# The second of two modulation chunks in the attention stage is summed by VectorE instead of the tensor engine

## The chip, the cores and the metric

The kernel runs on one core of one Trainium2 chip. The metric is the device time of one execution in microseconds (us); the time of a kernel is the median of several runs. Engines are named as the profile names them: PE is TensorE's matrix products and PEld its weight loads, DVE is VectorE, ACT is ScalarE, POOL is GpSimd and SP is SyncE, whose queue starts nearly all transfers.

## The reference

The reference is a trunk of two layers over 256 latent tokens and 256 context tokens of width 1024, in float32. Layer 0 mixes by attention (four differential heads and eight grouped-query heads), layer 1 by a bidirectional state-space scan; each is followed by a gated feed-forward block with a short convolution.

What matters here is the modulation. For each layer a vector of six chunks of 1024 numbers is computed from a conditioning vector, once for the latent tokens and once for the context:

```
mod   = silu(c)     @ mod_w[layer] + mod_b[layer]
mod_c = silu(c_ctx) @ mod_w[layer] + mod_b[layer]
sh1, sc1, g1, sh2, sc2, g2 = split(mod, 6)
h = rms_norm(x) * (1 + sc1) + sh1        # before the mixer
x = x + g1 * mixer(h)
h = rms_norm(x) * (1 + sc2) + sh2        # before the feed-forward block
x = x + g2 * ffn(h)
```

A chunk is written (layer, number): (0,0) and (0,1) are sh1 and sc1 of layer 0, (0,2) is g1, (0,3) is sh2, (0,4) is sc2, (0,5) is g2. (0,2) is needed when the output projection of attention is added to x; (0,3) and (0,4) are needed at the start of the first feed-forward block.

## The kernel before

Activations lie with channels on the 128 partitions and the 512 tokens in the free dimension. Every large product is made with weight blocks of 128 x 128. Float32 weights are split into a rounded half and a rest (L237 on ACT, L238 on DVE), and so are the activations; a step of a large product is then three products of 512 columns (L294, L295, L296). Weights come from memory in units of 8 blocks, 512 KB each. A unit lands in one of 5 raw buffers and is split into one of 2 split buffers.

The work is a list of units that `plan` writes: "w" for a unit of weights, "m" and "d" for the 1024 columns of one modulation chunk over 128 of the 1024 input channels. A chunk therefore has 8 units, each of 512 KB. `load_raw` starts their transfers from SP in the order of the list, a few units ahead of their use. The function `merge` spreads one list evenly between the members of another, `run` at a time. `run_units` goes through a phase of the list:

- a "w" unit does 8 steps of the current large product;
- an "m" unit goes to `mod_piece` (L396): four products on PE, one for each 256 columns, placed in four column groups of 32. The weights are the conditioning vectors, the moving data is the raw unit. The profile records each of these float32 products twice, so a unit is 8 records;
- a "d" unit goes to `mod_dve`: for each of the two conditionings DVE multiplies the 128 x 1024 raw unit by the vector's number of each partition and adds it to a running sum `macc` (L413 for the first unit, L415 for the others). After the eighth unit, 8 products with `pick` on PE (L423, 16 records) add the partitions up into four groups of rows.

Both ways end in `mod_evac`: a copy out of PSUM (L510), two transposes (L514), the bias (L519) and, for chunks 1 and 4, the norm's gain (L522).

The attention input projection ("ai") has 18 units of weights. The first 6 make six blocks of columns together and belong to the start phase. The other 12 make one block of 128 columns each: keys (ka), queries (qa) and values (va) of the four differential heads, in the order ka0 qa0 va0 ka1 qa1 va1 ka2 qa2 ka3 qa3 va2 va3. When a block of queries is done, its head's steps are queued with due times on a clock that the code keeps: `self.now` grows by 645 with each step of a large product, by as much with each of a head's scores, and by 420 with each "m" unit, and `service` takes one due task after every step and every modulation unit. A head has three groups of scores (L980 on PE, maxima L995 on DVE, exponentials L1000 on ACT), then normalisation on DVE (L1016; L1024 and L1026), transposes (L1042), their copies (L1045 on DVE, L1047 on ACT) and the product with the values (L1062). The next stage, the output projection ("ao", 8 units), takes the heads' outputs, the last head's at the end.

The calls of the code give a program order; a list scheduler then orders each engine's instructions at compile time with the program order as priority and its own estimates of time. Loads, splits and score products have a raised priority. On the chip every engine works off its list in that fixed order. Tiles of one tag share a fixed number of buffers, so a transfer or an instruction that opens a tile waits until a buffer is free. In this stage `macc` shares the tag k (6 buffers) with the five split key tiles, and all modulation products share one bank of PSUM.

In the attention stage two chunks, (0,2) and (0,4), are "m" units, in runs of four between the 12 weight units; (0,3) is summed by DVE in the output projection, and the other chunks by DVE in later stages.

Of the kernel before, what the change touches and what calls it, by code (L numbers as in the profile page):

```python
# [144 lines left out]
class Trunk:  # L145
# [15 lines left out]
    def plan(self):  # L161
        def w(name):
            n = len(ORDERS[name]) // UB
            return [("w", name, i) for i in range(n)]

        def mod(*chunks):
            return [("m", c, k) for c in chunks for k in range(KD)]

        def merge(ws, ms, first=0, last=0, run=1):
            res, j = list(ws[:first]), 0  # L170
            body = ws[first:len(ws) - last]
            for i, u in enumerate(body):
                res.append(u)
                while j < len(ms) and j * len(body) < (i + 1) * len(ms):
                    res += ms[j:j + run]
                    j += run
            return res + list(ws[len(ws) - last:])

        ai = w("ai")
        start, n = [("s", 0, 0), ("s", 0, 1)], 0  # L180
        for k in range(KD):
            while n * UB < 6 * (k + 1):
                start.append(ai[n])
                n += 1
            if k + 1 < KD:
                start += [("s", k + 1, 0), ("s", k + 1, 1)]

        def dve(*chunks):
            return [("d", c, k) for c in chunks for k in range(KD)]
        self.ph = {}  # L190
        self.ph["start"] = start
        self.ph["ai"] = merge(ai[n:], mod((0, 2), (0, 4)), run=4)
        self.ph["ao"] = merge(w("ao"), dve((0, 3)), last=3)
        self.ph["f0i"] = merge(w("f0i"), dve((1, 0), (1, 1), (0, 5)), first=FIRST, last=4)
        self.ph["f0o"] = merge(w("f0o"), dve((1, 3), (1, 4), (1, 2)), first=2, last=4)
        self.ph["si"] = w("si")
        self.ph["so"] = w("so")
        self.ph["f1i"] = merge(w("f1i"), dve((1, 5)), first=FIRST, last=4)
        self.ph["f1o"] = w("f1o")
        for n in ("start", "ai", "ao", "f0i", "f0o", "si", "so", "f1i", "f1o"):  # L200
            self.units += self.ph[n]
# [1363 lines left out]
```

## Time and profile before

| what | value |
| --- | --- |
| median of 3 runs | 1148.45 us (1147.38 to 1149.57) |
| profiled execution, its own time | 1148.3 us |
| span from first to last instruction | 1146.5 us |
| granted clock of TensorE, mean | 0.997 |
| PE, DVE, ACT busy over the span | 98%, 73%, 53% |
| records of L396 (the "m" units) | 128, from 78.2 to 195.5 us |
| sums of chunk (0,3) on DVE | 198.1 to 235.7 us |

How to read it: a page of the profile gives busy time of each engine; a busy PE is not a PE at its peak, since its products overlap and their ends are modelled. The chain is the work that ended last, followed back from the last instruction to what released each step. A group of waits such as "ACT ws L237 <- PE ai L296: 9.2, 6, 4.2" means that ACT's instructions of line 237 stood idle for products of line 296 for 9.2 us in all, 6 times, 4.2 us at most. In rows of the timeline a bracket gives the idle time before an instruction and what ended it. A row of a tile gives the durations as lowest/median/highest in ns and the first and last start in us.

### The profile page before, as it was taken

The numbers are of one execution on the slowest core, as the hardware profiler recorded it, in microseconds if no ns is written. First come the engines' busy times: TensorE is split into PE (matmuls) and PEld (weight loads), VectorE is DVE, ScalarE is ACT, GpSimd is POOL, SyncE is SP. The second block draws the span as 40 slices with busy tenths as digits, with TensorE's granted clock in tenths as the row PEclk, the third lists the DMA queues.
The fourth block names the chain that finished last, engine by engine and source line by source line (L and its number), as shares of the span: only waits on it lengthen the run. The fifth ranks groups of instructions, "written<-read, shape, count | busy, mean of one in ns | idle before, by whom it ended". The sixth has DMA issues, their size and how long they took to land.

```text
span 1146.5 us, 17295 instructions
## 1 busy us (share of the span) xinstructions
PE 1126.7 (98%) x6662; PEld 923.5 (81%) x6662; DVE 834.8 (73%) x1395; ACT 608.4 (53%) x1088; POOL 27.0 (2%) x37
## 2 busy tenths in 40 slices
PE   8999999999999999999999999999999999999997
PEld 4676666679888888888788988888778899999985
DVE  4567777966776877846556479999888779877645
ACT  4366666644433333333222468987677559655533
POOL 0000000000000000000000000000000101000000
PEclk9999999999999999999999999999999999999999
DMA  7744133433354555536566324454344366776661
GB/s 276 263 152 138 42 110 121 141 107 93 110 168 145 170 167 160 184 93 193 174 205 238 95 85 135 123 160 127 120 138 133 107 178 221 262 224 201 184 194 45
DMA packets 55858, 177.13 MB, mean 154 GB/s; under 512 B 5792, under 2 KB 14304, under 8 KB 55648
## 3 DMA queue, kind: packets, MB, share of 16 engines
q1 hardware_dynamic: 55488, 175.51, 48.6%
q8 instruction: 52, 0.85, 0.3%
q10 hardware_dynamic: 288, 0.52, 0.1%
q14 instruction: 30, 0.25, 0.1%
HBM read 174.89 MB, written 1.11 MB: 154 GB/s over the span
## 4 chain that ended last, share of the span: by engine, by line
PE 89%; DVE 5%; ACT 3%; DMA 2%; issue 1%; SPq 0%; DVEq 0%; ACTq 0%
PE f0i L294 7%; PE f0i L296 7%; PE f0i L295 7%; PE f1o L453 5%; PE f1i L296 4%; PE f1i L295 4%; PE f1i L294 4%; PE si L294 3%; PE si L296 3%; PE si L295 3%; PE f0o L294 3%; PE ai L294 3%; PE f0o L296 3%; PE f0o L295 3%; PE ai L296 3%; PE ai L295 3%
## 5 line engine op out<-in xcount | busy, mean ns | idle before, releaser
L237 ACT ACTIVATE ws<-raw 128x1024 fp32r<-128x1024 f32 x215 | 226.6, 1056 | 252.2 <-PE f0i L296 90.5
L238 DVE TENSOR_TENSOR ws<-raw,ws 128x1024 fp32r<-128x1024 f32 x215 | 262.4, 1222 | 96.5 <-ACT ws L237 95.6
L415 DVE SCALAR_TENSOR_TENSOR macc<-raw,cpad,macc 128x1024 f32<-128x1024 f32 x84 | 106.7, 1280 | 35.1 <-DMA raw<-mod_w 34.8
L294 PE MATMUL f0i<-h,ws 128*128 128x512 f32 x336 | 131.4, 391 | 0.0
L295 PE MATMUL f0i<-h,ws 128*128 128x512 f32 x336 | 130.8, 389 | 0.0
L296 PE MATMUL f0i<-h,ws 128*128 128x512 f32 x336 | 130.8, 389 | 0.0
L294 PE MATMUL si<-h,ws 128*128 128x256 f32 (+1 forms) x312 | 109.9, 352 | 0.6 <-DVE cacc L1158 0.6
L296 PE MATMUL si<-h,ws 128*128 128x256 f32 (+1 forms) x312 | 105.2, 337 | 3.1 <-DVE ws L238 3.1
L295 PE MATMUL si<-h,ws 128*128 128x256 f32 (+1 forms) x312 | 105.6, 338 | 0.0
L294 PE MATMUL f1i<-h,ws 128*128 128x256 f32 x288 | 82.1, 285 | 0.0
L296 PE MATMUL f1i<-h,ws 128*128 128x256 f32 x288 | 82.0, 285 | 0.0
L295 PE MATMUL f1i<-h,ws 128*128 128x256 f32 x288 | 81.5, 283 | 0.0
L294 PEld LDWEIGHTS f0i<-h,ws 128*128 128x128 f32 x336 | 63.1, 188 | 14.1 <-ACT hid L664 0.8
L296 PEld LDWEIGHTS f0i<-h,ws 128*128 128x128 f32 x336 | 63.1, 188 | 13.2
L295 PEld LDWEIGHTS f0i<-h,ws 128*128 128x128 f32 x336 | 63.1, 188 | 13.0
L296 PEld LDWEIGHTS si<-h,ws 128*128 128x128 f32 x312 | 59.0, 189 | 11.2 <-DVE ws L238 5.0
L294 PEld LDWEIGHTS si<-h,ws 128*128 128x128 f32 x312 | 59.1, 189 | 10.8 <-issue 4.6
L295 PEld LDWEIGHTS si<-h,ws 128*128 128x128 f32 x312 | 59.2, 190 | 5.4
L453 PE MATMUL f1o<-ws,hid 128*128 128x512 f32 (+1 forms) x276 | 60.7, 382 | 0.0
L294 PE MATMUL f0o<-hid,ws 128*128 128x512 f32 x154 | 60.6, 393 | 0.0
L294 PE MATMUL ai<-h,ws 128*128 128x512 f32 x144 | 58.8, 422 | 1.6 <-ACT h L654 1.5
L296 PE MATMUL f0o<-hid,ws 128*128 128x512 f32 x154 | 60.1, 390 | 0.0
(315 smaller groups left out, 2479.6 us busy)
## 6 DMA issues: line engine op xcount, KB each, us to landing
raw<-mod_w SPq DMA_DIRECT2D x80, 512.0 KB, 4.2
raw<-w_f0i SPq DMA_DIRECT2D x44, 512.0 KB, 4.0
raw<-w_f1i SPq DMA_DIRECT2D x44, 512.0 KB, 4.3
raw<-w_si SPq DMA_DIRECT2D x41, 512.0 KB, 3.6
raw<-w_f0o SPq DMA_DIRECT2D x22, 512.0 KB, 4.4
raw<-w_f1o SPq DMA_DIRECT2D x22, 512.0 KB, 3.5
raw<-w_ai SPq DMA_DIRECT2D x18, 512.0 KB, 3.7
raw<-mod_s SPq DMA_DIRECT2D x16, 512.0 KB, 5.2
```

What stands on the lines that cost most here:

```text
L237: ops = [nc.scalar.activation(out=hi, in_=r, func=AF.Copy)]
L238: ops.append(nc.vector.tensor_tensor(out=s[:, 1].rearrange("p a b -> p (a b)"), in0=r, in1=hi.bitcast(F32), op=ALU.subtract))
L294: nc.tensor.matmul(ps, lhsT=s[:, 0, b], rhs=xh[:, 0:n], start=first, stop=False)
L295: nc.tensor.matmul(ps, lhsT=s[:, 0, b], rhs=xl[:, 0:n], start=False, stop=False)
L296: nc.tensor.matmul(ps, lhsT=s[:, 1, b], rhs=xh[:, 0:n], start=False, stop=last)
L415: nc.vector.scalar_tensor_tensor(out=acc, in0=raw, scalar=sc, in1=acc, op0=ALU.mult, op1=ALU.add)
L453: nc.tensor.matmul(ps[:, c0 % 512:c0 % 512 + w], lhsT=hid[k][:, i, c], rhs=s[:, j].rearrange("p a b -> p (a b)")[:, c0:c0 + w], start=(k = ...
```

## The change

One line of `plan` changes. Chunk (0,2) stays on PE, in two groups of four; chunk (0,4) becomes "d" units and is spread one by one over the list that results.

```
-        self.ph["ai"] = merge(ai[n:], mod((0, 2), (0, 4)), run=4)
+        self.ph["ai"] = merge(merge(ai[n:], mod((0, 2)), run=4), dve((0, 4)))
```

Written out, with w6 to w17 for the units of weights, m2 for (0,2), m4 for (0,4) on PE and d4 for (0,4) on DVE, numbered from 0 to 7:

```
before: w6 [m2.0 m2.1 m2.2 m2.3] w7 w8 w9 [m2.4 m2.5 m2.6 m2.7] w10 w11 w12
        [m4.0 m4.1 m4.2 m4.3] w13 w14 w15 [m4.4 m4.5 m4.6 m4.7] w16 w17
after:  w6 d4.0 m2.0 m2.1 d4.1 m2.2 m2.3 w7 d4.2 w8 w9 d4.3 w10 w11 w12
        d4.4 m2.4 m2.5 d4.5 m2.6 m2.7 w13 d4.6 w14 w15 d4.7 w16 w17
```

`dve` makes the same units as `mod` with the letter "d" in place of "m". No other line differs; `mod_dve`, which the "d" units go to, is used as it stands.

## The prediction

> **What bounds the kernel now.** I read the page first, then the stretch of the attention stage by busy time, then its chain of waits in order of time, then the groups of waits of single engines. The page says that TensorE (PE) is on the chain almost everywhere:
>
> ```profile
> span 1146.5 us, 17295 instructions
> PE 1126.7 (98%) x6662; PEld 923.5 (81%) x6662; DVE 834.8 (73%) x1395; ACT 608.4 (53%) x1088; POOL 27.0 (2%) x37
> PE 89%; DVE 5%; ACT 3%; DMA 2%; issue 1%; SPq 0%; DVEq 0%; ACTq 0%
> ```
>
> The share of the span is an average, so the change has to be read from its own stretch. The units in question run between the end of the first six attention blocks (about 62 us) and the start of the output projection (about 216 us). Busy time by stretch (engine: us, then instructions):
>
> ```profile
> 62.00:216.00 154.00, 153.20 (x922) 104.11 (x921) 115.17 (x272) 100.46 (x214) 0.00 (x0) 1.00 0.34 110
> 160.00:180.00 20.00, 19.44 (x131) 12.30 (x129) 9.96 (x21) 12.85 (x26) 0.00 (x0) 1.00 0.38 132
> 180.00:200.00 20.00, 19.90 (x115) 13.67 (x108) 18.94 (x43) 10.77 (x24) 0.00 (x0) 1.00 0.54 165
> 200.00:216.00 16.00, 16.00 (x88) 12.25 (x87) 15.38 (x29) 10.87 (x23) 0.00 (x0) 1.00 0.49 157
> 216.00:240.00 24.00, 22.46 (x121) 16.69 (x120) 23.33 (x34) 14.58 (x30) 0.00 (x0) 1.00 0.48 143
> 300.00:480.00 180.00, 180.00 (x818) 147.53 (x818) 138.60 (x153) 65.48 (x84) 0.00 (x0) 1.00 0.52 161
> ```
>
> The columns are PE, its weight loads (PEld), VectorE (DVE), ScalarE (ACT). In 62 to 216 us PE is busy for 153.2 of 154 us and DVE for 115.2 of 154 (75%), so 38.8 us of DVE are free. But DVE's freedom is uneven: half of 160 to 180 us is free, while 180 to 240 us holds 57.65 of 60 us of DVE work. PE is therefore the bound with a DVE close behind it at the end of the stage.
>
> **What is removed.** The eight pieces of chunk (0,4) on PE are 64 of the 128 records at L396 (32 products, each recorded twice). In the chain, and once in the timeline beside it (the x30), they are:
>
> ```profile
> 145.46 0.55 PE modps L396 x2
> 161.72 1.93 PE L396 MATMUL modps<-raw,cpad 128*32 128x256 f32 x30
> 177.65 0.55 PE modps L396 x2
> 179.29 1.00 PE modps L396 x16
> 181.20 0.57 PE modps L396 x8
> 195.36 0.56 PE modps L396 x6
> ```
>
> 2+30+2+16+8+6 is 64 records, and their time is 0.55+1.93+0.55+1.00+0.57+0.56 = 5.16 us, of which 3.23 us stand on the chain itself (the burst of 30 runs beside a chain that goes through ACT and DVE there). So the removal is worth between 3.2 and 5.2 us of PE. Over the window from 0 to 262 us the chain gives the lines these shares, and L396 in it is both chunks together:
>
> ```profile
> by line: PE ai L294 13.5%; PE ai L296 12.2%; PE ai L295 12.1%; PE ov L1062 8.9%; PE s L980 7.2%; PE pT L1042 7.1%; PE ao L294 3.7%; PE ao L296 3.6%; PE ao L295 3.6%; PE modps L539 3.4%; PE modps L396 3.0%; DMA x<-x 2.1%; PE nsum L614 1.8%;
> ```
>
> 3.0% of 262 us are 7.9 us for two chunks, 3.9 us for one. I take 3.9 and keep 3.2 and 5.2.
>
> **What is added on PE.** A chunk summed on DVE needs the two picks that spread its sums to rows: 8 products, 16 records. The trace has them for chunk (0,3), on the chain, and DVE's part of the same chunk:
>
> ```profile
> 260.34 1.00 PE modps L423 x16
> L415 DVE SCALAR_TENSOR_TENSOR macc<-raw,cpad,macc x14: 1255/1278/1282, 200.9 to 234.4; 128x1024 f32<-128x1024 f32 x14
> L413 DVE TENSOR_SCALAR macc<-raw,cpad x2: 742/744/745, 198.1 to 198.7; 128x1024 f32<-128x1024 f32 x2
> ```
>
> That is +1.0 us of PE. Evacuation, transposes and bias (L510, L514, L519) stay what they are. **PE is relieved by 3.9 - 1.0 = 2.9 us**, with ends 2.2 and 4.2.
>
> **What is added on DVE.** 14 x 1.278 + 2 x 0.744 = 19.4 us. Against the 38.8 free us this leaves DVE at 134.6 of about 151 us, 89%. The engine takes its instructions in order, so the cost isn't the sum but what stands behind one: a maximum (L995), without which ACT can't take the exponentials, without which PE doesn't get its two score banks back. The nearest case is chunk (0,3), which runs in a DVE even fuller than this. Its chain at the end of attention:
>
> ```profile
> 218.99 0.69 DVE pTs L1045
> 219.69 0.60 DVE mx L995
> 220.28 3.21 DVE macc L415 x3
> 223.79 0.69 DVE mx L995
> 224.50 1.46 ACT e L1000 x4
> 221.36 1.12 PE L1062 MATMUL ov<-pTs,v 128*128 128x512 f32 x2 [0.74 <-ACT v L890]
> 226.00 0.97 PE L980 MATMUL s<-k,q 64*128 64x256 f32 x12 [0.70 <-ACT e L1000]
> ```
>
> Three sums in a row hold the maximum for 3.21 us, and PE loses 0.70 us to the exponentials and 0.74 us to a copy of ACT behind the same traffic: 1.4 us for a whole chunk. The lower bound for the new chunk is 0 (all in free time); below nothing is excluded, since no DVE instruction goes away. I take **1.4 us**: the DVE is emptier before 180 us, but score blocks come more often there. The upper bound is in the slow rival.
>
> **What moves.** Chunk (0,2)'s second half goes from behind the fourth of the stage's twelve weight units to behind the seventh. It is first read at L670. The rows below are, in order, from DVE's timeline, the groups of waits of ACT and of SyncE between 62 and 216 us, the tile k, and the chain:
>
> ```profile
> 254.54 2.44 DVE L670 SCALAR_TENSOR_TENSOR x<-ao,modT,x 128x256 f32<-128x256 f32 x6 [1.64 <-PE ao L296]
> ACT ws L237 <- PE ai L296: 9.2, 6, 4.2
> SPq L248 <- PE modps L396: 50.8, 10, 13.7
> L664 ACT ACTIVATE k<-qf x5: 627/634/635, 75.6 to 192.9; 128x512 fp32r<-128x512 f32 x5
> 144.12 0.91 PE s L980 x12
> ```
>
> The second half would be done near 165 us, some 90 us early, so I cost the move at nothing; without that cover it would hold back the residuals. The eight loads of (0,4) stand singly between weights in SyncE's queue instead of in fours. In this stretch SyncE waits for the L396 products to free a raw buffer; afterwards it waits for DVE's sums. The weights stand behind it, but the splits (L237) wait for PE to finish with the two split buffers (9.2 us) and no row of the stretch shows them waiting for a load, so a weight may land later at no cost; uncovered, a load is about 4 us. The two sums take two of the six k buffers. The seventh allocation then falls to the last k (192.9 us), which reuses that of the grouped heads, last scored near 144 us: 48 us of cover. The planner's clock loses 8 x 420 = 3360 of its nanoseconds, which by the code puts the later heads' steps up to two weight steps later in program order, that is 2 x 3 products of 0.23 us (three start in 253.18 to 253.88 us in a row below), 1.4 us of PE against the 3.9 us gone ahead of them: no cost on its own.
>
> **Sum.** -3.9 + 1.0 + 1.4 = -1.5 us. The profiled execution took 1148.3 us (span 1146.5 and 1.8 around it), 0.15 below the median of 1148.45, so 1146.8 us there and **1147.0 us** as a median.
>
> **Rivals.** *Full relief*: DVE's free time swallows the sums, as the 38.8 us allow. -2.9 to -4.2 us: 1144.3 to 1145.6. For it, PE's 153.2 of 154; against it, the 3.21 us row.
>
> *The gain is lost behind the last head.* The output of head 3 is ready in time by little:
>
> ```profile
> 251.55 0.63 ACT L664 ACTIVATE o<-of 128x512 fp32r<-128x512 f32 x1 [1.89 <-DVE of L1075]
> 252.22 0.69 DVE L665 TENSOR_TENSOR o<-of,o 128x512 fp32r<-128x512 f32 x1 [0.70 <-ACT o L664]
> 253.18 0.86 PE L294 MATMUL ao<-o,ws 128*128 128x512 f32 x3
> 253.88 0.40 PE L295 MATMUL ao<-o,ws 128*128 128x512 f32 x1
> ```
>
> The rounded half is there at 252.18 and first multiplied at about 253; the rest at 252.91 and first multiplied at 253.88. If DVE, full from 180 to 240 us, sets the date of head 3, PE comes 2.9 us sooner and finds nothing: 0.8 us is kept and the 1.4 us of stalls paid, 1148.45 - 0.8 + 1.4 = 1149.0. Against it: steps of the fifth output block, independent of head 3, can stand in.
>
> *PE isn't the bound in this stage.* Its weight loads are busy for 104.11 of 154 us, 68%, less than DVE's 75%; if that is the truer measure, the products that go away were filling gaps, the relief is worth nothing and the stalls remain: 1148.45 + 1.4 = 1149.9. Against it: from 300 to 480 us, where PE has no gap at all, the same share is only 147.53/180 = 82%, and the many short products of this stage must lower it. The Trainium skill, "Perfetto Trace Analysis", section "Identifying the Most-Contended Engine", takes this side: it holds that matmul busy time misjudges TensorE because matmuls are pipelined, and that the busy share of weight loads should be read instead, by which DVE would be the engine to relieve here and not to load.
>
> *Slower: DVE waits in line for its raws.* In the next stage the sums often stand at DVE's head before the load has landed:
>
> ```profile
> DVE macc L415 <- DMA raw<-mod_w: 16.3, 13, 1.9
> DVE macc L413 <- DMA raw<-mod_w: 3.2, 1, 3.2
> ```
>
> At 16.3/13 = 1.25 us and 3.2 us for the first, eight pieces stand for 3.2 + 7 x 1.25 = 12 us. In the next stage nothing of it reaches PE; behind score blocks 0.70 of 3.21 us (22%) did, and half is my upper guess. That makes 2.6 to 6.0 us beyond the sum, +1.1 to +4.5, middle 1151.3. It decides once more than 1.5 us of those waits reach PE. Against it: DVE's groups of waits from 190 to 262 us, where (0,3) is summed, hold no such row, and raws are loaded several units ahead.
>
> **How the numbers follow.** Partial relief (forecast) 0.42, full relief 0.20, gain lost behind the last head 0.13, PE not the bound 0.07, slower 0.18. What this measurement tells from no change is 0.2%, 2.3 us: below 1146.15 or above 1150.75. Faster: all of full relief and some 0.12 of the forecast's lower edge, 0.32. Slower: 0.13 of the slow rival and 0.03 of the two before it, 0.16. The rest is 0.52. The range runs from full relief's end, 1144.0, to just past the slow rival's middle, 1151.5; the forecast's own is 1145.6 to 1148.5.
>
> **What would show it.** L396 with 64 records instead of 128 and L423 with 16 more before 216 us; PE's busy time from 62 us to head 3's output shorter by about 3 us while DVE's grows by 19.4. The stall term is right if waits of PE for ACT's e and DVE's mx grow by 1 to 2 us in total; the lost gain, if a wait for ACT's o appears in front of the output projection's last products; the slow rival, if DVE shows rows "macc <- DMA" between 62 and 216 us. I am wrong if the stage after 262 us starts later than before, or if the gain comes from anywhere but the missing products.

## The result and the profile after

The changed kernel takes **1168.04 us** (median of 4 runs, 1166.44 to 1169.84) against 1148.35 us (4 runs), a ratio of 1.017 with a 95% interval of 1.0151 to 1.019. It is 19.7 us slower; the forecast was 1147.0 us, the range 1144.0 to 1151.5. The profiled execution took 1166.44 us.

The page of the changed kernel: span, busy time of the engines, and the chain's shares.

```profile
span 1164.7 us, 17220 instructions
PE 1129.6 (97%) x6614; PEld 925.5 (79%) x6614; DVE 852.8 (73%) x1411; ACT 608.4 (52%) x1088; POOL 27.0 (2%) x37
PE 78%; DVE 11%; ACT 5%; DMA 4%; issue 2%; SPq 0%; DVEq 0%; POOL 0%; ACTq 0%; POOLq 0%
```

The records fell by 48 on PE (64 gone, 16 added) and DVE is busy 18.0 us longer. But PE's share of the chain fell from 89% to 78%, and DVE, ACT and DMA took it. PE's busy time *grew* by 2.9 us although products were taken away: the same products took longer somewhere.

Where the time went is dated by the first product of the next stage, which follows 0.1 us behind the last one of the output projection. First before, then after (the tile f0i; durations in ns, then first and last start in us):

```profile
L358 PE MATMUL f0i<-zero x4: 377/378/389, 279.8 to 280.8; 128*128 128x512 bf16 x4
```

```profile
L358 PE MATMUL f0i<-zero x4: 377/378/389, 296.1 to 297.1; 128*128 128x512 bf16 x4
```

This date is called the **stage's end** below. 16.3 of the 18.2 us that the span grew by lie ahead of it; all that follows is only 1.9 us longer. The start phase, which is the same work in all the kernels of this text, doesn't end on the same date in every execution, though: its last transposes, before and after, start at

```profile
L548 PE MATMUL modps<-cst,modsb x32: 165/251/272, 15.9 to 59.7; 128*128 128x2 f32 x32
```

```profile
L548 PE MATMUL modps<-cst,modsb x4: 166/251/251, 58.1 to 58.4; 128*128 128x2 f32 x4
```

The time from there to the stage's end is called the **stage's length**. It covers the rest of the input projection, the heads and the output projection, and it grew from 279.8 - 59.7 = 220.1 to 296.1 - 58.4 = 237.7 us, by 17.6.

Busy time by stretch, before, then after (columns as in the prediction, then the granted clock, the share of the DMA engines and their GB/s; the sum is over eleven stretches that cover 62 to 296 us, and the two short stretches at the end are no part of it):

```profile
80.00:100.00 20.00, 20.00 (x105) 15.44 (x102) 16.92 (x44) 12.04 (x23) 0.00 (x0) 1.00 0.54 167
...
sum 234.00, PE 231.65 PEld 169.49 DVE 174.92 ACT 143.53 POOL 2.98; mean PE 21.06 PEld 15.41 DVE 15.90 ACT 13.05 POOL 0.27
```

```profile
80.00:100.00 20.00, 15.79 (x67) 11.19 (x66) 15.71 (x32) 10.18 (x17) 0.00 (x0) 0.83 0.62 199
...
160.00:180.00 20.00, 16.86 (x97) 10.01 (x96) 14.24 (x33) 12.62 (x34) 0.00 (x0) 1.00 0.09 26
...
200.00:220.00 20.00, 17.14 (x84) 11.65 (x83) 19.33 (x33) 11.00 (x19) 0.00 (x0) 1.00 0.41 121
220.00:240.00 20.00, 17.98 (x87) 12.55 (x87) 18.98 (x32) 9.27 (x24) 0.00 (x0) 0.91 0.39 118
...
sum 234.00, PE 217.71 PEld 154.88 DVE 177.54 ACT 130.35 POOL 0.00; mean PE 19.79 PEld 14.08 DVE 16.14 ACT 11.85 POOL 0.00
...
83.70:90.50 6.80, 4.95 (x11) 3.49 (x12) 4.38 (x12) 4.34 (x6) 0.00 (x0) 0.50 0.66 214
220.30:223.70 3.40, 3.40 (x20) 2.85 (x19) 2.81 (x4) 2.33 (x6) 0.00 (x0) 0.50 0.68 188
```

PE stood still for 234 - 217.71 = 16.3 us in place of 2.35, that is 13.9 us more, spread over nearly all of the stage. In two stretches its granted clock was 0.5: half of the 4.95 + 3.40 us that it was busy there, 4.2 us, is lost as well. 13.9 + 4.2 less the forecast relief of 2.9 is 15.2 us of the 17.6; the rest is not accounted for.

**The first stall.** PE's timeline of the changed kernel:

```profile
82.85 0.64 PE L396 MATMUL modps<-raw,cpad 128*32 128x256 f32 x8 [2.16 <-DMA raw<-mod_w]
85.51 0.80 PE L294 MATMUL ai<-h,ws 128*128 128x512 f32 x1 [2.02 <-ACT ws L237]
...
87.79 0.63 PE L295 MATMUL ai<-h,ws 128*128 128x512 f32 x1
88.22 0.63 PE L296 MATMUL ai<-h,ws 128*128 128x512 f32 x1
...
90.69 0.39 PE L296 MATMUL ai<-h,ws 128*128 128x512 f32 x1
90.92 0.39 PE L294 MATMUL ai<-h,ws 128*128 128x512 f32 x1
```

PE waits 2.16 us for a load of modulation and then 2.02 us for the split of a unit of weights; from 87.4 to 90.3 us its products start every 0.43 us, and later every 0.23 again. Why the load is late stands in SyncE's timeline (the second number runs from the first to the last issue of a row), before and after:

```profile
56.34 1.28 SPq L248 DMA_DIRECT2D raw<-mod_w  x3
63.90 15.28 SPq L248 DMA_DIRECT2D raw<-w_ai  x3
```

```profile
54.99 24.33 SPq L248 DMA_DIRECT2D raw<-mod_w  x5
79.42 0.37 SPq L248 DMA_DIRECT2D raw<-w_ai  x1
```

Before, the weight w7 is asked for at 63.90 us, after only at 79.42. In the list six modulation units now stand in front of it, where there were four (the first of them is issued ahead of these rows), and there are five raw buffers. The last of the six has to wait until PE's first products of L396, at 76.8 us, free a buffer, because the two that belong to the new sums free none: DVE doesn't touch them for a long time (DVE's timeline of the changed kernel):

```profile
92.09 0.68 DVE L665 TENSOR_TENSOR k<-qf,k 128x512 fp32r<-128x512 f32 x1
92.69 0.75 DVE L413 TENSOR_SCALAR macc<-raw,cpad 128x1024 f32<-128x1024 f32 x1
```

The first sum starts as soon as the rest (what the rounding leaves) of a key tile is written: that of ka0, the second of the five, since the grouped heads' keys were written at 74.84 us. Both tiles are of the tag k, and the sums' tiles are opened behind that of ka0. Whether this is the cause is tried in own_tag and raw_own.

**The later stalls.** Behind these stand maxima and not loads. The groups of waits from 56 to 290 us, before, then after:

```profile
ACT e L1000 <- DVE mx L995: 8.3, 5, 2.5
ACT e L1000 <- DVE mx L998: 8.2, 8, 2.3
...
PE s L980 <- ACT e L1000: 1.0, 2, 0.7
```

```profile
ACT e L1000 <- DVE mx L998: 13.6, 9, 3.4
...
ACT e L1000 <- DVE mx L995: 10.5, 7, 2.5
...
PE s L980 <- ACT e L1000: 5.3, 4, 2.6
...
PE nsum L614 <- DVE rstd L605: 2.6, 1, 2.6
```

and the chain of the changed kernel passes through a sum, the rest of a head's output (L665) and two maxima before the exponentials may start:

```profile
118.34 1.28 DVE macc L415
119.62 0.60 DVE o L665
120.22 1.20 DVE mx L995 x2
121.58 1.20 ACT e L1000 x4
```

### The profile page after: what moved, and what is told of

Its sections match the earlier page's. It is cut to its first block, busy times and chain, and to the rows that moved or that the text cites. A ratio compares the mean times of both kernels' runs of the same rounds, so it can differ in the third digit from the quotient of the medians.

```text
span 1164.7 us, 17220 instructions
## 1 busy us (share of the span) xinstructions
PE 1129.6 (97%) x6614; PEld 925.5 (79%) x6614; DVE 852.8 (73%) x1411; ACT 608.4 (52%) x1088; POOL 27.0 (2%) x37
## 4 chain that ended last, share of the span: by engine, by line
PE 78%; DVE 11%; ACT 5%; DMA 4%; issue 2%; SPq 0%; DVEq 0%; POOL 0%; ACTq 0%; POOLq 0%
PE f0i L294 7%; PE f0i L296 7%; PE f0i L295 7%; PE f1o L453 5%; DVE ws L238 3%; PE f0o L294 3%; PE f0o L296 3%; PE f0o L295 3%; PE ai L294 3%; PE si L296 2%; PE si L294 2%; PE si L295 2%; PE ai L295 2%; PE ai L296 2%; DMA cumb<-cumd 2%
## 5 line engine op out<-in xcount | busy, mean ns | idle before, releaser
L237 ACT ACTIVATE ws<-raw 128x1024 fp32r<-128x1024 f32 x215 | 226.6, 1055 | 257.2 <-PE f0i L296 93.3
L415 DVE SCALAR_TENSOR_TENSOR macc<-raw,cpad,macc 128x1024 f32<-128x1024 f32 x98 | 124.6, 1279 | 36.2 <-DMA raw<-mod_w 35.9
L294 PE MATMUL f0i<-h,ws 128*128 128x512 f32 x336 | 131.4, 391 | 0.0
L294 PE MATMUL si<-h,ws 128*128 128x256 f32 (+1 forms) x312 | 109.9, 352 | 0.6 <-DVE cacc L1158 0.6
L294 PE MATMUL f1i<-h,ws 128*128 128x256 f32 x288 | 82.1, 285 | 0.0
L294 PEld LDWEIGHTS f0i<-h,ws 128*128 128x128 f32 x336 | 63.1, 188 | 14.1 <-ACT hid L664 0.8
L294 PEld LDWEIGHTS si<-h,ws 128*128 128x128 f32 x312 | 59.1, 190 | 10.7 <-issue 4.6
L294 PE MATMUL ai<-h,ws 128*128 128x512 f32 x144 | 59.6, 427 | 4.3 <-ACT ws L237 2.0
L294 PE MATMUL f0o<-hid,ws 128*128 128x512 f32 x154 | 60.5, 393 | 0.0
```

Source lines behind the costliest of these rows:

```text
L237: ops = [nc.scalar.activation(out=hi, in_=r, func=AF.Copy)]
L294: nc.tensor.matmul(ps, lhsT=s[:, 0, b], rhs=xh[:, 0:n], start=first, stop=False)
L415: nc.vector.scalar_tensor_tensor(out=acc, in0=raw, scalar=sc, in1=acc, op0=ALU.mult, op1=ALU.add)
```

## The experiments

Two theories were put against each other at first: the *sums* cost the time (they stand in DVE's order in front of maxima), or the *held raw buffers* do (the units wait for DVE, and the weights behind them are late). Later runs ask what the relief of PE was worth and where. In the kernels with "none", and in those with "no3", chunk (0,4) or (0,3) is left out and its rows are set to 1.

| kernel | what is different | median us | ratio to before (95%) | stage's end us | start phase's last L548 us | stage's length us |
| --- | --- | --- | --- | --- | --- | --- |
| before | | 1148.35 | | 279.8 | 59.7 | 220.1 |
| after | the change | 1168.04 | 1.0151 to 1.019 | 296.1 | 58.4 | 237.7 |
| none | (0,4) left out | 1149.45 | 1.0002 to 1.0037 | 283.3 | 59.3 | 224.0 |
| dve_only | after, sums without loads | 1161.14 | 1.0074 to 1.0119 | 289.0 | 57.2 | 231.8 |
| raw_only | after, loads with hardly any sums | 1162.2 | 1.0084 to 1.0142 | 289.4 | 57.6 | 231.8 |
| own_tag | after, sums in a tag of their own | 1165.33 | 1.0113 to 1.0169 | 293.4 | 57.5 | 235.9 |
| raw_own | raw_only and own_tag | 1152.7 | 1.0015 to 1.0042 | 282.9 | 58.5 | 224.4 |
| dve_half | dve_only, each long sum in two halves | 1160.36 | 1.0077 to 1.0121 | 286.5 | 58.8 | 227.7 |
| same_places | (0,4) on DVE, in the places of before | 1161.1 | 1.0064 to 1.0145 | 291.7 | 57.3 | 234.4 |
| no3 | before, (0,3) left out | 1145.44 | 0.9962 to 0.9995 | 275.7 | 58.7 | 217.0 |
| no3_none | before, (0,3) and (0,4) left out | 1145.14 | 0.9955 to 0.9993 | 270.9 | 57.2 | 213.7 |
| after_no3 | after, (0,3) left out | 1162.33 | 1.0101 to 1.0168 | 293.3 | 60.8 | 232.5 |
| d3_on_pe | before, (0,3) on PE | 1151.03 | 1.0002 to 1.0035 | 282.4 | 59.6 | 222.8 |
| late3 | before, sums of (0,3) begin later | 1146.3 | 0.9966 to 0.999 | 279.7 | 61.0 | 218.7 |

A ratio is to executions of before that were timed beside the kernel; their medians lie between 1147.5 and 1149.6 us. The medians carry what happens in later stages too. The span from the stage's end on is 866.7 us before and 866.0 to 869.2 in most kernels, but 871.8 in dve_only, 874.5 in raw_only and 876.7 in dve_half, whose later stages are written as before. The granted clock explains a part: half of the time that it stood at 0.5 behind the stage's end is 1.6 us before and 4.4, 5.0 and 7.6 us in these three. The rest isn't settled; so the parts of the attention stage are compared by its length, which is that of one execution of each kernel.

Executions of one kernel differ by their clock, too, and that can be estimated for all of them: each has its span and its mean granted clock, and span x (1 - clock) is, from above, what the half speed cost (from above, since PE wasn't busy all that time). Its median is 3.4 to 4.6 us in the executions of before, 9.2 in none and 11.1 in after. What is left, span x clock, is 1142.4 to 1142.6 us for before on all four occasions, 1139.1 for none and 1155.0 for after. The clock is on record to 0.001, which is 1.1 us or so.

**None: neither sums nor loads.** What is the relief of PE worth alone?

```
-        self.ph["ai"] = merge(merge(ai[n:], mod((0, 2)), run=4), dve((0, 4)))
+        self.ph["ai"] = merge(ai[n:], mod((0, 2)), run=4)
```

> Chunk (0,4) is left out altogether: no units, no loads, no sums, no picks (its scale is a constant 1); chunk (0,2) stays on PE in two groups of four. It gives the price of the whole chunk as it stands on PE in the kernel before, the most that any move of it can gain. By my prediction's rows 3.2 to 5.2 us: 1143 to 1145. If DVE or loads bind the stage instead of PE: within 2 us of the kernel before, 1146 to 1150.

Nothing, or less than nothing: the 3.2 to 5.2 us of gain don't come, the median is 0.2% above before, and in the profiled execution the stage ends 3.5 us *later* than before and is 3.9 us longer.

```profile
L358 PE MATMUL f0i<-zero x4: 376/378/389, 283.3 to 284.3; 128*128 128x512 bf16 x4
```

The products of the input projection are done 6.3 us sooner (208.7 against 215.0 us), but the last head's output is written at 251.7 against 252.2. In between the chain is DVE's, filled with the sums of (0,3), which begin only 2.9 us sooner (195.24 against 198.1 us):

```profile
195.24 1.41 DVE macc L413 x2
196.65 1.04 DVE macc L415
...
199.04 1.97 DVE macc L415 x2
```

PE runs out of work, and after the pauses its clock falls. Two stretches, which overlap:

```profile
210.00:220.00 10.00, 7.69 (x35) 4.57 (x34) 9.60 (x16) 2.84 (x7) 0.00 (x0) 0.83 0.34 105
216.60:226.80 10.20, 9.04 (x26) 4.85 (x28) 7.88 (x8) 3.62 (x9) 0.00 (x0) 0.50 0.32 101
```

10.2 us at half the clock with 9.04 us of PE's work in it are 4.5 us lost, more than the relief. This execution, with 1151.38 us, is slower than the median of its ten, but they say the same by the estimate above: without the clock's part none is 3.3 us below before (1139.1 against 1142.4), which is near the 3.9 us that the prediction read for (0,4) on PE, and the clock's part is 5.8 us larger (9.2 against 3.4). So the relief is there, by this estimate, and the clock behind the new pauses costs more.

**dve_only and raw_only: the two halves of the cost.** In the first DVE sums a resident tile, so that nothing is loaded for (0,4); in the second the units are loaded and released by DVE, but all sums after the first unit run over 2 of 1024 columns (both leave the right value of the chunk out).

```
-        self.ph["ai"] = merge(merge(ai[n:], mod((0, 2)), run=4), dve((0, 4)))
+        self.ph["ai"] = merge(merge(ai[n:], mod((0, 2)), run=4), [("x", c, k) for _, c, k in dve((0, 4))])
...
-                (self.mod_piece if u[0] == "m" else self.mod_dve)(u[1], u[2], self.take())
+                raw = self.h[u[2]].rearrange("p a b -> p (a b)").bitcast(F32) if u[0] == "x" else self.take()
+                (self.mod_piece if u[0] == "m" else self.mod_dve)(u[1], u[2], raw)
```

> The changed kernel, but the eight d units of chunk (0,4) load nothing: DVE makes the same 16 sums at the same places of the program from a resident 128x1024 tile of activations, and the picks follow (chunk (0,4) then holds other numbers). It takes away the raw buffers that the d units hold and their loads, and keeps all 19.4 us of DVE work. Theory R (weights come late because d units hold raw buffers until DVE gets to them): the wait of PE for the seventh unit's split near 83 to 85 us goes, and the time falls by 8 us or more, to 1148 to 1160. Theory D (the sums stand in DVE's line before the maxima and copies of the heads): the time stays within 4 us of the changed kernel's, 1164 to 1172.

```
+                c4 = slice(0, 2 if ch == (0, 4) else 1024)
+                nc.vector.scalar_tensor_tensor(out=acc[:, c4], in0=raw[:, c4], scalar=sc, in1=acc[:, c4], op0=ALU.mult, op1=ALU.add)
```

> The changed kernel, but after the first unit of chunk (0,4) DVE sums only 2 of the 1024 columns, so 14 sums of 1.28 us become short ones; loads, raw buffers, tiles and the order of the units stay (chunk (0,4) is wrong in the other columns). Theory R: raw buffers are still held until DVE's first sum, which comes behind the first key tile of the tag k, so the wait near 83 to 85 us stays and the time is 1156 to 1168. Theory D: 14 x 1.2 = 17 us of DVE work are gone and the time is 1145 to 1151.

The tile f0i in dve_only, then in raw_only:

```profile
L358 PE MATMUL f0i<-zero x4: 377/378/389, 289.0 to 290.1; 128*128 128x512 bf16 x4
```

```profile
L358 PE MATMUL f0i<-zero x4: 376/378/389, 289.4 to 290.4; 128*128 128x512 bf16 x4
```

By the stage's length, the sums by themselves cost 7.8 us against none (231.8 against 224.0) and the loads by themselves 7.8 too. With none's 3.9 that is 19.5 us for the 17.6 of the change; by the medians the two are 11.7 and 12.8 us above none's. So the parts overlap, the split is rough, and each is a large cost by itself: neither theory alone is enough. dve_only's time lies between the ranges of both theories; raw_only's is in that of the held buffers. raw_only keeps the late weight: its SyncE issues five units of modulation from 54.18 to 78.52 us and the weight at 78.62.

**own_tag and raw_own: why the buffers are held.** The sums get two buffers of their own, and the keys keep four.

```
-            self.acct, self.accn = ("k", "k"), K_BUFS
+            self.acct, self.accn = ("mk", "mk"), 2
...
-K_BUFS = 6
+K_BUFS = 4
```

> The changed kernel, but the running sums of the attention stage have a tag of their own with 2 buffers, and the tag k has 4 instead of 6. The first sums need then not wait for the tile of the first keys (ka0) to be opened: the program places them near 58 us and 64 us instead of 92.7 us, and raw buffers are given back sooner. Theory R: no wait of PE for a split near 83 us, 1150 to 1160 (some 8 to 18 us below the changed kernel). Theory D: the DVE work is the same, so within 4 us of the changed kernel, 1164 to 1172.

> The run with short sums (2 of 1024 columns after the first unit) and, as well, the running sums under a tag of their own (2 buffers; the tag k has 4). DVE has hardly any of the new work left and may open the sums before the first key tile, so each raw buffer goes back as soon as it has landed; loads and their order stay those of the changed kernel. If the raw buffers cost what they do because the first sum is late (at 92.9 us in the run without the own tag), the half-speed stretch near 82 us goes, the feed-forward block starts near the 283.3 us of the run without chunk (0,4), and the time is 1148 to 1153. If the eight extra loads and their place in SyncE's queue are the cost, it stays at 1158 to 1165.

In raw_own the first sum is at 56.6 us (92.9 in raw_only), SyncE hands out the weight w7 at 63.34 us in place of 78.62, and the cost of the loads is gone. SyncE's timeline and the tile f0i of raw_own:

```profile
55.12 7.89 SPq L248 DMA_DIRECT2D raw<-mod_w  x5
63.34 0.33 SPq L248 DMA_DIRECT2D raw<-w_ai  x1
```

```profile
L358 PE MATMUL f0i<-zero x4: 377/378/390, 282.9 to 284.0; 128*128 128x512 bf16 x4
```

The stage's length is 224.4 us, none's 224.0, and the ratios to before agree within their intervals. So the late weight is owed to the raw buffers held behind the key tile's place in the shared tag, and not to the bytes. With the sums at full length, in own_tag, the weight is early too (64.52 us), and the stall at 80 us has gone, but only 1.8 us of the stage come back: other modulation units now come late at 100 us, behind a DVE that was busy 19.27 of the 20 us before. The time is in the range that was expected if the sums are the cost. The groups of waits of PE in own_tag, 56 to 290 us:

```profile
PE modps L396 <- DMA raw<-mod_w: 3.0, 3, 2.2
PE s L980 <- ACT e L1000: 2.9, 3, 2.1
```

The clock takes a part of the gain: it stands at 0.5 for 20.4 us of the stage, against 10.2 in after. By the estimate without the clock's part own_tag is 5.5 us below after (1149.5 against 1155.0); the ratios themselves can't be told apart by their intervals.

**dve_half: is it the length of one sum?** dve_only with each long sum in two halves of 512 columns, so that a maximum between them waits half as long.

```
-                nc.vector.scalar_tensor_tensor(out=acc, in0=raw, scalar=sc, in1=acc, op0=ALU.mult, op1=ALU.add)
+                for c4 in ((slice(0, 512), slice(512, 1024)) if ch == (0, 4) else (slice(0, 1024),)):
+                    nc.vector.scalar_tensor_tensor(out=acc[:, c4], in0=raw[:, c4], scalar=sc, in1=acc[:, c4],
+                                                   op0=ALU.mult, op1=ALU.add)
```

> The run with sums from resident data, but each of the 14 long sums of chunk (0,4) in two halves of 512 columns (28 sums of about 0.65 to 0.75 us, in all some 1 to 3 us more DVE work). If the cost of the sums is what stands in line behind a single one (head of line), the halves let maxima and copies in between and the feed-forward block starts 2 to 5 us sooner than 289.0 us; time 1154 to 1159. If it is DVE's total work, the start is the same or 1 to 3 us later; 1160 to 1165.

A half takes more than half of a whole sum's 1278 ns (tile macc of dve_half):

```profile
L417 DVE SCALAR_TENSOR_TENSOR macc<-h,cpad,macc x28: 721/742/748, 93.8 to 146.2; 128x512 f32<-128x512 f32 x28
```

The stage ends 2.5 us sooner in the profiled execution (286.5 against 289.0) and is 4.1 us shorter, with 6.8 us at half the clock in place of 10.2; the ratio to before doesn't move. That the length of a single sum is a part of the 7.8 us is likely by that execution and not established by the times.

**same_places: is it the spreading?** The eight units on DVE in two runs of four, at the places that the change took them from.

```
-        self.ph["ai"] = merge(merge(ai[n:], mod((0, 2)), run=4), dve((0, 4)))
+        self.ph["ai"] = merge(ai[n:], mod((0, 2)) + dve((0, 4)), run=4)
```

> Chunk (0,4) is summed by DVE, but its units stand where they stood on PE, in two runs of four behind the seventh and the tenth of the twelve weight units before which they stood (w12 and w15), and chunk (0,2) ends behind w12 no longer but behind w9, as in the kernel before. Only the engine differs from the kernel before. Theory R (late weights): no d unit stands ahead of w7, so the half-speed stretch near 84 us goes, but a run of four holds four of five raw buffers until DVE has summed them; 1153 to 1161. Theory D (DVE work alone): 1160 to 1168.

1161.1 us, some 7 us better than the change and still 1% slower than before; the ranges of the two theories overlap there, so the time doesn't decide between them. The first sum is at 183.7 us, although SyncE has issued the first four units by 110.5 us; so they hold four of the five raw buffers until then. The 62 to 140 us are as full as before (77.98 of 78 us on PE), and the whole loss lies behind: 4.1 us idle from 140 to 180 and 7.3 from 180 to 220 us, where DVE is busy 39.67 of 40 us, and the mean clock of these two stretches is 0.96 and 0.84. The spreading decides where it is paid, and a part of how much.

**no3, no3_none, after_no3: is DVE too full with two chunks?** (0,3) is left out of before, of none's counterpart, and of after.

```
-        self.ph["ao"] = merge(w("ao"), dve((0, 3)), last=3)
+        self.ph["ao"] = w("ao")
```

> The kernel before without chunk (0,3): no d units in the output projection, its shift is a constant 1. DVE loses 19.4 us of sums from 198 to 236 us and PE 1.0 us of picks. Theory H (the last head's date is set by DVE, which these sums fill): the last head's output comes 2 to 6 us sooner than 252.2 us, but PE still has all its work, so the time is 1145 to 1147. If the heads' own chain sets that date: unchanged, 1147 to 1149.

> Neither chunk (0,3) nor chunk (0,4) is computed (constants). Against the run without (0,3) alone it shows what the PE time of (0,4) is worth once no sums fill DVE at the end of the heads. Theory H: 3 to 5 us less than without (0,3) alone, 1140 to 1143. If the relief of PE is worth nothing for another reason (the heads' own chain): within 1.5 us of it.

> The changed kernel without the sums of chunk (0,3) (its eight units, loads and picks are left out and its rows set to 1; all else as changed). It asks whether the 16 us are owed to the sums of (0,4) and (0,3) together filling DVE at the end of the stage, or arise before (0,3) begins. Theory A, local: the held raw buffers and the sums in front of maxima cost their time at 80 to 160 us whatever follows; then taking (0,3) away gives back only what it gave in the kernel before (4 us at the first product of f0i, 9 us at the last head's output): f0i starts at about 292, the median is about 1164, 1.4% above before. Theory B, one full DVE: without (0,3) DVE has 19.4 us of room again and the change costs no more than it does PE good; f0i starts at 276 to 281, the median is 1146 to 1151. In between, 282 to 288: both, and the part given back beyond 4 us is the share of the second.

The tile f0i in no3, no3_none and after_no3:

```profile
L358 PE MATMUL f0i<-zero x4: 377/378/389, 275.7 to 276.8; 128*128 128x512 bf16 x4
```

```profile
L358 PE MATMUL f0i<-zero x4: 376/378/389, 270.9 to 272.0; 128*128 128x512 bf16 x4
```

```profile
L358 PE MATMUL f0i<-zero x4: 377/378/389, 293.3 to 294.4; 128*128 128x512 bf16 x4
```

Without (0,3) the last head's output is written 9.0 us sooner (243.2 against 252.2), and now taking (0,4) from PE brings the stage's end 4.8 us forward. Of these, 1.5 us come from the start phase; the stage is 3.3 us shorter, and PE keeps its full clock through all of it in both. In these two executions the relief is worth what PE is spared, and that speaks for the sums of (0,3) as what makes none's relief worthless. The medians don't show it: those of no3 and no3_none differ by 0.3 us only, over 6 to 7 us of scatter each. The profiled execution of no3_none is the fastest of its ten (1141.93 us, clock 0.998); the slowest took 1148.69 us at a clock of 0.991.

after_no3 says the rest: the change makes the stage 232.5 - 217.0 = 15.5 us longer even where DVE has the 19.4 us of (0,3) free, nearly as much as the 17.6 with (0,3) in. (By the stage's end it is 17.6 against 16.3 us, but after_no3's start phase ended 2.1 us later than no3's, with 10.2 us at half the clock against 3.4.) Its weight is asked for at 81.85 us, and PE is busy 15.39 of 20 us from 80 to 100. DVE's total load at the end of the stage is not what makes the change dear, as the theory called local expected. The sums and the held buffers do most of it at their own places.

**d3_on_pe and late3: the other direction.** (0,3) on PE instead of DVE; and (0,3) left on DVE, its units beginning behind the third weight unit of the output projection and not behind the first.

```
-        self.ph["ao"] = merge(w("ao"), dve((0, 3)), last=3)
+        self.ph["ao"] = merge(w("ao"), mod((0, 3)), last=3)
```

> The opposite change: the kernel before with chunk (0,3) on PE in the output projection, one m unit at a time, in place of DVE's sums. PE +4 to +5 us for the products and -1.0 for the picks, DVE -19.4 us between 198 and 236 us. Theory H: the end of the heads is no longer held by sums, and the PE products fill waits there: 1145 to 1149. If PE is the bound there: +3 to +4 us, 1151 to 1152.

```
-        self.ph["ao"] = merge(w("ao"), dve((0, 3)), last=3)
+        self.ph["ao"] = merge(w("ao"), dve((0, 3)), first=3, last=2)
```

> The kernel before, with chunk (0,3)'s d units behind the fourth to sixth of the eight weight units of the output projection instead of from the first: the sums come later, when the heads need DVE less. By the runs without chunk (0,3) its sums hold the last head's output back by 9 us (252.2 against 243.2 us) but cost the stage only 4.1 us, 1.0 of them its picks. If later sums set the last head free: 1144.5 to 1147. If PE has no work to fill the time with, or the picks become late for the feed-forward block: 1147.5 to 1150.

d3_on_pe has the early last head (243.6 us) and no idle PE (65.98 of 66 us from 216 to 282 us), and its stage is 2.7 us longer than before: there PE is the bound, and the 2.9 us of products are paid nearly in full. late3 measures 0.9978 of before, a gain of some 2.5 us, the only kernel with the whole computation that is faster than both. Its profiled execution had 10.2 us at half the clock in the start phase against 3.4 before; the stage ends at 279.7 us, as before, but is 1.4 us shorter. Where the rest of the gain comes from isn't shown.

## Why the prediction was wrong

- **The removal and its size: right; what it is worth: wrong.** L396 has 64 records left, L423 got its 16, and DVE 19.4 us of sums. But "PE is relieved by 3.9 - 1.0 = 2.9 us" was entered at full value. The run without (0,4) has a stage 3.9 us longer than before and a median 0.2% above it. The rival "the gain is lost behind the last head" had this mechanism, with DVE setting that head's date, and it got 0.13; its answer, that the steps of the fifth output block stand in, is not enough to keep PE's clock: 10.2 us at 0.5. The sign set for that rival, a wait of the output projection's products for ACT's o, appears neither in none nor in after. The rival by weight loads, "PE isn't the bound in this stage", has the same outcome, but in the profiled executions without (0,3) the relief does shorten the stage by 3.3 us, so there PE's products count.
- **The stall term: 1.4 us was forecast, some 7.8 us of the stage measured** (dve_only against none). It was taken from three sums late in (0,3), where few score blocks are left, and the free 38.8 us of DVE were held to cover the rest. An average share of free time says nothing of what a sum stands in front of: the waits of exponentials for maxima grew from 16.5 to 24.1 us, and PE's for exponentials from 1.0 to 5.3. "1 to 2 us in total" was the test set for this step, and it failed.
- **"A weight may land later at no cost": the step that failed outright.** w7 was asked for 15.5 us later, and the row of waits for splits, absent before, appeared: "PE ai L294 <- ACT ws L237" with 2.0 us. The prediction did see that the weights stand behind the sums in SyncE's queue, but took the absence of a wait in the *old* order for cover in the new one. The price is 7.8 us of the stage (raw_only against none).
- **The tag k: the wrong end was looked at.** The seventh allocation had its 48 us of cover. What cost was an early one: the sums' tiles come behind that of ka0, so DVE's first sum stood until 92.69 us while its loaded units kept two of five buffers. With a tag of their own the first sum is at 55.3 us, and with short sums as well 0.4 of the 7.8 us are left.
- **The slow rival: the side was right, the mechanism wrong.** DVE did not wait in line for its raws: from 56 to 235 us there is one such wait of 0.8 us. It was the other way round, the raws waited for DVE. Its price, at most 6.0 us, counted only one side of the queue.
- **No term for the clock.** The granted clock of before was 1.00 in every stretch that I quoted, and the sum took it as given. After the change it was 0.5 for 10.2 us of the stage, 4.2 us of cost; in none the clock alone outweighs the relief. The Trainium skill, "TensorE: Matmul & The Clock Gate", Part 1, says that PE falls to half the rate after about one window of 3.4 us without work and needs as long to come back. The trace agrees with the half rate and with the length of the stretches, 6.8 and 3.4 us. But PE wasn't without work for 3.4 us ahead of them: the pauses were 2.16 us, and 2.6 us before the second, and PE was still busy for 1.04 of the 3.4 us from 80.3 to 83.7 and for 0.81 of those from 216.9 to 220.3.
- **The second half of (0,2)** was done by 138 us and not near 165, and cost nothing. "I am wrong if the stage after 262 us starts later than before" is what happened: 16.3 us.

## What to carry to other kernels

A slow consumer that shares a small ring of load buffers with the critical stream must be costed by how long it *holds* a buffer, counted from the load to its first instruction, and the first tile it opens decides that as much as the last; ask of every "nothing waits here now" what the new order puts ahead of it. Work moved to an engine with free time has to be placed against the reductions that others wait for, since its free share is an average. And a relief of the busiest engine is worth what the next date behind it allows: leave the work out entirely once, as in none, before pricing its move, and see what the pauses that it opens do to the clock.

## What the hardware showed

PE's granted clock changed only on a grid. In each of the 14 traces all its changes between 1.0 and 0.5 lie whole multiples of 3.413 us apart, within 0.1 us (in after at 83.7, 90.5, 220.3 and 223.7 us: 2, 40 and 41 steps from the first), and the place of the grid against the program differs from execution to execution. With the traces cut along it, every stretch at full clock in which PE was busy for less than 49% was followed by one at half clock and none above 81% was; between the two, both happened. The clock came back only after a stretch with PE busy for 90% or more. So the same pauses can cost nothing or a good deal: the start phase, the same work in all, had no half clock in dve_only, 3.4 us of it before and 10.2 in late3. In none, pauses of 1.09, 0.16 and 0.48 us and the beginning of a fourth, from 213 to 216.6 us, stood ahead of 10.2 us at half the clock, 4.5 us of loss.

Halving a long sum on DVE took 742 ns in place of 639, so that two halves are 16% dearer than the whole.
